# Moving the residual and the gated expert bias of a mixture-of-experts block into its last expert, and reordering the routing on TensorE

## The chip, the cores and the metric

The kernel runs on one core of one Trainium2 chip. The metric is the device time of one execution in microseconds (us). The kernel was timed in 3 runs, and one more execution was profiled. The engines are TensorE (PE; its weight loads are listed as PEld), VectorE (DVE), ScalarE (ACT), GpSimd (POOL) and SyncE (SP), whose queue issues nearly all transfers from HBM.

## What is computed

One layer of a diffusion backbone on 256 latent tokens and 256 context tokens of 1024 values, all float32. Cut to what the change touches:

```python
mod_l = silu_c @ w_mod + b_mod                      # 6 x 1024
sh1, sc1, g1, sh2, sc2, g2 = split(mod_l)
ml  = token_mixer(modulate(x, sh1, sc1), ...)       # scans, pooling, projections
xl  = layer_norm(alpha * x + g1 * ml, ln1_g, ln1_b)
h   = modulate(xl, sh2, sc2)
# mixture of experts: top 4 of 32, softmax over the chosen logits
logits = h @ router_w + router_b
gates  = softmax over top_k(logits, 4)              # 0 elsewhere
for e in range(32):
    gu  = h @ w1[e] + b1[e]
    a   = min(gu[:, :D], 7); l = clip(gu[:, D:], -7, 7)
    out += gates[:, e] * ((a * sigmoid(1.702 * a) * (l + 1)) @ w2[e] + b2[e])
xl = layer_norm(alpha * xl + g2 * out, ln2_g, ln2_b)
```

## The kernel before

**Weights.** All weights come through 20 blocks of SBUF of 1 MB each (128 partitions by 2048 floats): a ring of 12, and eight more that the first part of the kernel gives up when it no longer needs them (`donate`). The list `plan` fixes the order of the transfers: modulation, input projection, output projection, the last modulation part `("mod", 5, q)`, then for each expert in turn eight blocks of `w1` and, one expert later, four of `w2`. A block is freed when the last matmul that reads it has been written (`free`, `retire`), and each freed block lets SP's queue issue the next transfer of the plan. SP takes its transfers strictly in order, and each waits for the engines that last used its block.

**First part (L253 to L762).** Layer norms, modulation, scans, pooling and the output projection. Its instructions run on each engine in the order in which the code is written. It ends with the routing (L727 to L762): `project` is the output projection, `normalise(h)` the first layer norm of the token half h (it leaves the normalised tokens, without gain and bias, in `xn`), `turn1(h)` transposes `xn` on PE, `route(h)` makes from the transposed tokens `h2T` (modulated, four tiles by DVE and four by ACT), `xaT` (alpha times the first layer norm's output, eight tiles by ACT) and the router's logits `lp`; `top4a` and `top4b` pick the four experts on DVE (`selb`, `ge`), `place(h)` counts on PE where each token stands in its expert's queue, and `residual(h)` starts the four PSUM accumulators `acc[t][h]` with `xaT`, turned back by a matmul with the identity. `gemv(5)` computes the last modulation part g2; it is added to its bias row and spread to four groups of 32 partitions (`bp`, L751, copied to `g2s`).

**Experts (L764 to L1111).** Tokens go in groups of 32. The table `SEQ` says how many groups each of 32 experts, sorted by load, is given (56 groups in all); four groups make a page, and a pass takes one or two groups of one expert. A pass is: `gemm1` over eight `w1` blocks (with `hooks`, small pieces of other work after the k-th block, in PE's order), the bias `b1` by matmuls (L881), `swiglu` on DVE and ACT, and then, for the pass before it, `gemm2` over four `w2` blocks into the PSUM tile `py`, whose result DVE scales by `g2s` into `Y` (L929). `combine` adds a page's `Y` to `acc` with the gates as stationary operand. In pass 1 `arrange_a` and `arrange_b` sort the experts' maps, `arrange_b` also makes masked `b2` times g2 in `Y`, and `arrange_c` (L978, four matmuls of 128x512, right before `gemm2` of pass 0) adds gates times b2 to `acc`.

**End.** In the pass of the last expert (`p == NE - 1`), when the plan is empty, `spread` (L233) lays the second layer norm's gain and bias out over all partitions, `lngb`, by four pairs of matmuls and four ACT copies through one PSUM tile (`misc`, a single buffer). Then come `gemm1` of the last expert, `gemm2` of the last but one, `gemm2` of the last, the last `combine` and `last_norm`.

Of the kernel before, what the change touches and what calls it, by code (L numbers as in the profile page):

```python
# [18 lines left out]
P = 128  # L19
# [37 lines left out]
def hybrid(tc, a, out):  # L57
# [136 lines left out]
    AB = const.tile([P, 2, KD], F32, name="AB")  # L194
    aln = const.tile([P, 2, KD], F32, name="aln")
    posm = const.tile([P, 2, NE], F32, name="posm")
# [9 lines left out]
    keyc = const.tile([P, 2], F32, name="keyc")  # L206
    lnrow = const.tile([P, 2, T], F32, name="lnrow")
    pool.memset(lnrow, 0.0)
# [44 lines left out]
    with ExitStack() as px:  # L253
# [84 lines left out]

        gsel = sb.tile([GW, 3, P], F32, tag="gsel", name="gsel")
        for h in range(2):  # L340
# [24 lines left out]

        def gemv(v):
            gp = ps.tile([P, T], F32, tag="gv", name="gp")
            for q in range(4):
# [12 lines left out]
                free(("mod", v, q))  # L381
            return gp
# [46 lines left out]
        dve.tensor_scalar(hgb, col(C_GA, 16), 0.5, None, op0=ALU.mult)  # L429
        dve.tensor_scalar(aln, col(C_LG, 2 * KD).rearrange("p (i k) -> p i k", i=2), ALPHA, None, op0=ALU.mult)  # L430
        lam = col(C_LAM, 8)
# [181 lines left out]

        h2T, xaT = (block("aa")[:, D * i : D * i + D].rearrange("p (k t) -> p k t", k=KD) for i in range(2))
        eq = sb.tile([P, 2, NE], F32, name="eq")
# [31 lines left out]
        def route(h, trs):  # L647
            for j in range(KD):
                src = trs[j // 4][:, j % 4, :]
                if j >= 4:  # L650
                    act.activation(
                        h2T[:, j, :], src, AF.Identity, bias=AB[:, 1, j : j + 1], scale=AB[:, 0, j : j + 1]
                    )
                else:
                    dve.tensor_scalar(
                        h2T[:, j, :], src, AB[:, 0, j : j + 1], AB[:, 1, j : j + 1], op0=ALU.mult, op1=ALU.add
                    )
            for j in range(KD):
                src = trs[j // 4][:, j % 4, :]
                act.activation(  # L660
                    xaT[:, j, :], src, AF.Identity, bias=aln[:, 1, j : j + 1], scale=aln[:, 0, j : j + 1]
                )

            if h:
                lp = ps.tile([P, NE], F32, tag="gv", name="lp")
            else:
                lp = mm.tile([P, NE], F32, tag="mm", name="lp")
# [11 lines left out]
        def top4b(h):  # L679
            lh, gh, eh, ch, nh = lg[:, h, :], ge[:, h, :], eq[:, h, :], cum[:, h, :], ng[:, h : h + 1]  # L680
            v4 = mx[:, h, 3:4]
            dve.tensor_scalar(eh, lh, v4, None, op0=ALU.is_equal)
            dve.tensor_tensor_scan(ch, one, eh, 0.0, op0=ALU.mult, op1=ALU.add)
            dve.tensor_reduce(nh, gh, axis=AX.X, op=ALU.add)
            dve.tensor_scalar(nh, nh, -1.0, 4.0, op0=ALU.mult, op1=ALU.add)
            dve.scalar_tensor_tensor(ch, ch, nh, eh, op0=ALU.is_le, op1=ALU.mult)
            dve.tensor_tensor(gh, gh, ch, op=ALU.add)
            dve.tensor_copy(selb[:, h, :], gh)

# [24 lines left out]

        def residual(h):
            for j in range(KD):
                half, j4 = j // 4, j % 4
                pe.matmul(  # L718
                    acc[h][half][:, P * j4 : P * j4 + P],
                    xaT[:, j, :],  # L720
                    ident,
                    start=(j4 == 0),
                    stop=False,
                    skip_group_check=True,
                )

        project(0, (4, 5, 6, 7))  # L727
# [21 lines left out]
        bp = mm.tile([P, T], F32, tag="mm", name="bp")  # L749
        for c in range(4):  # L750
            pe.matmul(  # L751
                bp[32 * c : 32 * c + 32, :],
                ident[:, 32 * c : 32 * c + 1].to_broadcast([P, 32]),
                bgrow[:, 1, :],
                start=True,
                stop=True,
                skip_group_check=True,
            )
        act.activation(g2s, bp, AF.Copy)
        softmax_a(1)  # L760
        place(1)
        donate("aa")  # L762
    order = ExitStack()
# [57 lines left out]
    def maps(page):  # L821

        Pm = wk.tile([P, 2, P], F32, name="Pm")
# [67 lines left out]
    def swiglu(ph, av):  # L891
        sgm = wk.tile([P, T], F32, name="sgm")
# [37 lines left out]

    def combine(Y, PgT, t, h, lo=0, hi=512):

# [30 lines left out]
    def arrange_b():  # L963
# [4 lines left out]
        dve.tensor_copy(placed, so)  # L968
        ahead = page_maps(1)
        for c in range(4):  # L970
            dve.scalar_tensor_tensor(
                Y[:, T * c : T * c + T], b2, col(C_MASK + c), g2s, op0=ALU.mult, op1=ALU.mult
            )

    def arrange_c():
        for h in range(2):
            for t in range(2):
                pe.matmul(  # L978
                    acc[t][h],
                    GT[:, 2 + t],  # L980
                    Y[:, 512 * h : 512 * h + 512],
                    start=False,
                    stop=False,
                    skip_group_check=True,
                )
# [187 lines left out]
def _layout(inp):  # L1173
# [47 lines left out]
    def emb(n):  # L1221
# [42 lines left out]
```

## Time and profile before

| what | value |
|---|---|
| time, median of 3 runs | 1105.54 us (1105.21 to 1105.77) |
| time of the profiled execution | 1105.46 us |
| its span, first to last instruction | 1103.8 us |
| PE busy | 980.9 us, 89% of the span |
| DVE / ACT / POOL busy | 300.2 / 164.6 / 54.9 us |
| read from HBM | 442.25 MB, 402 GB/s over the span |
| mean granted TensorE clock | 0.954 of 2.4 GHz |
| chain of work that ended last | PE 55%, DMA 42% |

The span is 1.7 us shorter than the time of the same execution; what lies outside it is taken as fixed. Over most of the span the 16 DMA engines are at work throughout, and PE's busy time holds many waits for weights; the first fifth and the last 30 us are different stages with limits of their own, so shares over the whole span say little about them.

### The profile page before, as it was taken

To read this page: it belongs to the slowest core of one execution; us is meant where nothing else is said; L and a number is where in the kernel's file an instruction comes from. 1 tells how busy PE (TensorE), PEld (TensorE's weight loads), DVE (VectorE), ACT (ScalarE), POOL (GpSimd) and SP (SyncE) were. 2 spreads that over 40 slices of the span, in tenths; PEclk is the share of its full clock that TensorE was granted. 3 is DMA by queue.
4 is the path that set the end of the run, shared out by engine and by line. 5 is a ranking of instruction groups with operands and counts; after the bars stand their busy time and mean duration, and the time that the engine had idled before them with its cause. 6 is when DMAs were issued, how large, how long until landed. Compare 5 with 4: busy or idle time off the path is not lost.

```text
span 1103.8 us, 21803 instructions
## 1 busy us (share of the span) xinstructions
PE 980.9 (89%) x9237; PEld 420.1 (38%) x9238; DVE 300.2 (27%) x803; ACT 164.6 (15%) x347; POOL 54.9 (5%) x73
## 2 busy tenths in 40 slices
PE   7899999999999968699998897969999887999774
PEld 3356654434444313243433242324343233444222
DVE  4436562231313211213312112212221221223114
ACT  3245342101111000101010010000101010110011
POOL 2128200000000000000000000000000000000001
PEclk9899999999999989989998998989999998999886
DMA  9999689999999999999999999999999999999993
GB/s 366 355 404 374 260 348 379 376 422 424 422 424 423 423 424 424 424 425 424 423 424 424 424 423 424 423 425 423 424 422 425 425 423 424 425 423 414 424 422 135
DMA packets 89861, 444.76 MB, mean 403 GB/s; under 512 B 9304, under 2 KB 15576, under 8 KB 56992
## 3 DMA queue, kind: packets, MB, share of 16 engines
q1 hardware_dynamic: 89528, 443.01, 97.4%
q8 instruction: 74, 1.21, 0.4%
q10 hardware_dynamic: 232, 0.32, 0.1%
q14 instruction: 27, 0.22, 0.1%
HBM read 442.25 MB, written 1.05 MB: 402 GB/s over the span
## 4 chain that ended last, share of the span: by engine, by line
PE 55%; DMA 42%; DVE 2%; ACT 0%; issue 0%; ACTq 0%; SPq 0%; DVEq 0%
DMA blk<-in_w_dram 40%; PE ph L867 22%; PE py L916 12%; PE zp L458 5%; PE misc L847 3%; DMA blk<-in_w_mod_dram 2%; PE acc L604 2%; PE acc L933 2%; PE ph L881 2%; PE gp L373 1%; PE acc L488 1%; PE misc L906 1%; PE bp L233 1%; DMA cols<-in_cols_dram 0%; PE misc L857 0%; PE acc L718 0%
## 5 line engine op out<-in xcount | busy, mean ns | idle before, releaser
L867 PE MATMUL ph<-blk,xe 128*32 128x512 f32 x3584 | 430.4, 612 | 40.1 <-DMA blk<-in_w_dram 38.9
L916 PE MATMUL py<-blk,aT 128*32 128x256 f32 x3584 | 221.8, 400 | 54.5 <-DMA blk<-in_w_dram 49.8
L867 PEld LDWEIGHTS ph<-blk,xe 128*32 128x32 f32 x3584 | 104.2, 111 | 281.5 <-issue 176.3
L916 PEld LDWEIGHTS py<-blk,aT 128*32 128x32 f32 x3584 | 117.0, 115 | 170.8 <-issue 56.6
L929 DVE TENSOR_TENSOR Y<-py,g2s 32x256 f32<-32x256 f32 x224 | 94.2, 420 | 232.1 <-PE py L916 229.3
L894 DVE TENSOR_SCALAR av<-ph 128x256 f32<-128x256 f32 x56 | 23.6, 422 | 463.6 <-PE ph L881 463.6
L907 ACT ACTIVATE aT<-misc 128x256 f32<-128x256 f32 (+1 forms) x38 | 18.4, 485 | 386.2 <-PE misc L906 386.2
L850 ACT ACTIVATE xe<-misc,AB 128x128 f32<-128x128 f32 x108 | 40.7, 457 | 167.9 <-PE misc L847 167.9
L847 PEld LDWEIGHTS misc<-Pm,blk 128*128 128x128 f32 x432 | 51.4, 195 | 23.8 <-issue 23.8
L458 PE MATMUL zp<-blk 128*128 128x256 f32 (+1 forms) x192 | 59.2, 465 | 1.1 <-DVE blk L425 1.1
L847 PE MATMUL misc<-Pm,blk 128*128 128x128 f32 x432 | 56.5, 285 | 1.1 <-DVE Pm L826 1.1
L881 PE MATMUL ph<-b,SM 128*32 128x512 f32 x448 | 56.8, 609 | 0.0
L895 ACT ACTIVATE sgm<-av 128x256 f32<-128x256 f32 x56 | 23.3, 417 | 212.1 <-DVE av L894 212.1
L933 PE MATMUL acc<-Y,PgT 128*128 128x512 f32 (+1 forms) x120 | 51.9, 576 | 0.5 <-DVE Y L929 0.5
L1139 POOL TENSOR_TENSOR blk<-blk 128x512 f32<-128x512 f32 (+1 forms) x2 | 2.0, 995 | 941.7 <-ACT blk L1138 940.9
L458 PEld LDWEIGHTS zp<-blk 128*128 128x128 f32 x192 | 37.1, 195 | 22.6 <-issue 17.6
L933 PEld LDWEIGHTS acc<-Y,PgT 128*128 128x128 f32 x120 | 21.4, 189 | 31.3 <-issue 21.9
L881 PEld LDWEIGHTS ph<-b,SM 128*32 128x32 f32 x448 | 15.0, 114 | 35.7 <-issue 35.7
L604 PE MATMUL acc<-blk 128*128 128x512 f32 x64 | 27.8, 592 | 0.0
L897 DVE SCALAR_TENSOR_TENSOR av<-l,av 128x256 f32<-128x256 f32 x56 | 23.8, 426 | 10.8 <-ACT sgm L895 9.6
L373 PE MATMUL gp<-blk,csil 128*32 128x256 f32 x384 | 22.6, 381 | 2.1 <-DMA blk<-in_w_mod_dram 2.1
L906 PEld LDWEIGHTS misc<-ident,av 128*128 128x128 f32 x112 | 11.9, 144 | 32.9 <-issue 32.1
(214 smaller groups left out, 459.6 us busy)
## 6 DMA issues: line engine op xcount, KB each, us to landing
blk<-in_w_dram SPq DMA_DIRECT2D x383, 1024.0 KB, 19.6
blk<-in_w_mod_dram SPq DMA_DIRECT2D x23, 1024.0 KB, 10.6
blk<-in_w_in_dram SPq DMA_DIRECT2D x6, 1024.0 KB, 16.0
blk<-in_w_out_dram SPq DMA_DIRECT2D x4, 1024.0 KB, 5.3
blk<-in_ctx_dram SPq DMA_DIRECT2D x2, 512.0 KB
blk<-in_x_dram SPq DMA_DIRECT2D x2, 512.0 KB
blk<-in_w_mod_dram SPq DMA_DIRECT2D x2, 512.0 KB, 16.2
blk<-in_w_dram SPq DMA_DIRECT2D x2, 512.0 KB
```

What stands on the lines that cost most here:

```text
L373: pe.matmul(gp[32 * c : 32 * c + 32, :], csil[:, k, :], w[:, kk, T * c : T * c + T], start=(k == 0), stop=(k == KD - 1), skip_group_check= ...
L458: pe.matmul(zp[:, :n], w[:, k, P * half : P * half + P], hT(k)[:, :n], start=(k == 0), stop=(k == KD - 1))
L604: pe.matmul(acc[h][half], mixT[:, k, P * h : P * h + P], weight("out", k // 2)[:, k % 2, 512 * half : 512 * half + 512], start=(k == 4), s ...
L847: pe.matmul(gx[:, kk], xn[:, t, P * k : P * k + P], Pm[:, t], start=(t == 0), stop=(t == 1))
L850: act.activation(xe[:, k], gx[:, kk], AF.Identity, bias=AB[:, 1, k : k + 1], scale=AB[:, 0, k : k + 1])
L867: pe.matmul(ph[32 * c : 32 * c + 32], x[:, k], wv[:, :, c, :], start=(k == 0), stop=False, skip_group_check=True,)
L881: pe.matmul(ph[32 * c : 32 * c + 32], sel[c].to_broadcast([P, GS]), b1, start=False, stop=True, skip_group_check=True,)
L894: dve.tensor_scalar(av, ph[:, 0, :], 7.0, None, op0=ALU.min)
L897: dve.scalar_tensor_tensor(av, l1, 8.0, av, op0=ALU.min, op1=ALU.mult)
L916: pe.matmul(py[32 * c : 32 * c + 32, i], aT[:, i, k % 2, k // 2, :], W[k // 2][:, k % 2, T * c : T * c + T], start=(k == 0 and i == 0), st ...
L929: dve.tensor_tensor(dst[:, T * c : T * c + T], py[r, i], g2s[r], op=ALU.mult)
L933: pe.matmul(acc[t][h][:, lo:hi], PgT[:, P * t : P * t + P], Y[:, 512 * h + lo : 512 * h + hi], start=False, stop=False, skip_group_check=True,
```

## The change

- `residual` is no longer made in the routing: `xaT`, its sixteen ACT instructions, its sixteen matmuls of 128x128 and the table `aln` are gone. The accumulators are now started by the first `combine_all` (page 1, `start=True`).
- In the last expert's pass, four freed blocks are taken. `spread` first lays out the *first* layer norm's gain and bias (`ln1`, from two more rows of `lnrow`); DVE makes alpha times (`xn` * gain + bias) in token order, in four instructions of 128x1024 (`residual`), and then masked b2 times g2 into another block (`add_b2`, four of 128x256). Hooks of `gemm1` put the following into PE's order: after block 0 gates times b2 (four matmuls of 128x512), after blocks 2 and 4 the two `spread`s of the second layer norm's gain and bias, after block 5 the residual, by four matmuls of 128x512 with the identity.
- `arrange_c` and the b2 part of `arrange_b` are gone from pass 1.
- In the routing, three quarters of `gemv(5)` run where all of it ran; the fourth quarter runs after the second half's logits. The bias row of g2 is added by a matmul with the identity instead of by DVE, and ACT copies the sum to `g2r`. `top4b(0)` moves ahead of `turn1(1)` and `route(1)`, both `softmax_a` behind `top4b(1)`, and the spreading of g2 (`bp`) behind `place(1)`. `donate("aa")` moves to behind `route(1)`.
- `selb` is written by its own addition ahead of `ge`, not copied from it. `Pm` and `sgm` have one buffer instead of two, `gsel` shares a buffer, `lp` always comes from the pool `mm`.

```diff
-        g2p = gemv(5)
-        dve.tensor_tensor(bgrow[:, 1, :], g2p, bgrow[:, 1, :], op=ALU.add)
+        g2p = gemv(5, (0, 1, 2))
+        top4b(0)
         trs = turn1(1)
-        residual(0)
         lp = route(1, trs)
-        top4b(0)
+        donate("aa")
+        gemv(5, (3,), g2p)
+        pe.matmul(g2p, ident, bgrow[:, 1, :], start=False, stop=True, skip_group_check=True)
+        g2r = s2.tile([P, T], F32, tag="part", name="g2r")
+        act.activation(g2r, g2p, AF.Copy)
         place(0)
-        residual(1)
-        softmax_a(0)
         top4a(1, lp)
         top4b(1)
+        softmax_a(0)
+        softmax_a(1)
+        place(1)
...
+    def add_b2(Yb):
         for c in range(4):
             dve.scalar_tensor_tensor(
-                Y[:, T * c : T * c + T], b2, col(C_MASK + c), g2s, op0=ALU.mult, op1=ALU.mult
+                Yb[:, T * c : T * c + T], b2, col(C_MASK + c), g2s, op0=ALU.mult, op1=ALU.mult
             )
-    def arrange_c():
         for h in range(2):
             for t in range(2):
+                combine(Yb, GT[:, 2:4].rearrange("p t n -> p (t n)"), t, h)
+
+    def residual(ln1, R):
+        for h in range(2):
+            dve.scalar_tensor_tensor(R[:, h], xn[:, h], ALPHA, ln1[:, 0], op0=ALU.mult, op1=ALU.mult)
+            dve.scalar_tensor_tensor(R[:, h], ln1[:, 1], ALPHA, R[:, h], op0=ALU.mult, op1=ALU.add)
+
+    def add_residual(R):
+        for t in range(2):
+            for h in range(2):
                 pe.matmul(
+                    acc[t][h], ident, R[:, t, 512 * h : 512 * h + 512], start=False, stop=False, skip_group_check=True
                 )
...
-        if not plan and lngb is None:
-            lngb = block(slots.pop(0)).rearrange("p (i n) -> p i n", i=2)
+        if p == NE - 1:
+            tags = [slots.pop(0) for _ in range(4)]
+            lngb, ln1, y2 = (block(tag).rearrange("p (i n) -> p i n", i=2) for tag in tags[:3])
+            Yb = block(tags[3])[:, 0:D]
             for r in range(2):
-                spread(None, lnrow[:, r, :], wk, ps, "misc", lngb[:, r, :])
+                spread(None, lnrow[:, 2 + r, :], wk, ps, "misc", ln1[:, r, :])
+            residual(ln1, y2)
+            hooks[0] = lambda: add_b2(Yb)
+            for r in range(2):
+                hooks[2 + 2 * r] = lambda r=r: spread(None, lnrow[:, r, :], wk, ps, "misc", lngb[:, r, :])
+            hooks[5] = lambda: add_residual(y2)
```

PE in the routing, before: `lp` are the logits of the two halves, `gp` is `gemv(5)`, `tr` the transposes, `acc<-ident,blk` the residual, `pp` the counts, `bp` the spreading of g2.

```order
L669 MATMUL lp<-cols,blk 128x32 x8
L373 MATMUL gp<-blk,csil 32x256 x32
L643 MATMUL tr<-ident,blk 128x128 x8
L718 MATMUL acc<-ident,blk 128x128 x8
L669 MATMUL lp<-cols,blk 128x32 x8
L695 LDWEIGHTS tri
L695 MATMUL pp<-selb,tri 128x32
L718 MATMUL acc<-ident,blk 128x128 x8
L751 MATMUL bp<-bgrow,ident 32x256 x4
```

The same place now:

```order
L659 MATMUL lp<-cols,blk 128x32 x8
L372 MATMUL gp<-blk,csil 32x256 x24
L641 MATMUL tr<-ident,blk 128x128 x8
L659 MATMUL lp<-cols,blk 128x32 x8
L372 MATMUL gp<-blk,csil 32x256 x8
L722 MATMUL gp<-bgrow,ident 128x256
L685 LDWEIGHTS tri
L685 MATMUL pp<-selb,tri 128x32
L684 LDWEIGHTS one_305
```

Both residuals are gone, and the last quarter of `gp` with its bias now stands between the second logits and the first count; `bp` has moved out of this stretch, to behind the second count.

DVE in the same stretch, with the semaphores that each instruction waits for, down to the second half's logits (`lg<-lp,cols`): `blk<-tr,AB` are DVE's four tiles of the second half's `h2T`, and `eq` to `selb` is the pick of the first half's experts. Before:

```order
L655 TENSOR_SCALAR blk<-tr,AB 128x128 [waits PE_49]
L655 TENSOR_SCALAR blk<-tr,AB 128x128 x3
L682 TENSOR_SCALAR eq<-lg,mx 128x32
L683 SCALAR_TENSOR_TENSOR cum<-one,eq 128x32 [waits DVE_49]
L684 TENSOR_REDUCE ng<-ge 128x1
L685 TENSOR_SCALAR ng<-ng 128x1 [waits DVE_49]
L686 SCALAR_TENSOR_TENSOR cum<-cum,ng,eq 128x32 [waits DVE_49]
L687 TENSOR_TENSOR ge<-ge,cum 128x32 [waits DVE_49]
L688 CAST selb<-ge 128x32 [waits DVE_49]
L709 SCALAR_TENSOR_TENSOR posm<-pp,ge 128x32 [waits PE_49]
L238 TENSOR_SCALAR lg<-lg,mx 128x32
L674 TENSOR_TENSOR lg<-lp,cols 128x32
```

And now:

```order
L672 TENSOR_SCALAR eq<-lg,mx 128x32
L673 SCALAR_TENSOR_TENSOR cum<-one,eq 128x32 [waits DVE_49]
L674 TENSOR_REDUCE ng<-ge 128x1
L675 TENSOR_SCALAR ng<-ng 128x1 [waits DVE_49]
L676 SCALAR_TENSOR_TENSOR cum<-cum,ng,eq 128x32 [waits DVE_49]
L677 TENSOR_TENSOR selb<-ge,cum 128x32 [waits DVE_49]
L678 TENSOR_TENSOR ge<-ge,cum 128x32 [waits DVE_49]
L653 TENSOR_SCALAR blk<-tr,AB 128x128 [waits PE_49]
L653 TENSOR_SCALAR blk<-tr,AB 128x128 x3
L699 SCALAR_TENSOR_TENSOR posm<-pp,ge 128x32 [waits DVE_49,PE_49]
L664 TENSOR_TENSOR lg<-lp,cols 128x32
```

The pick of the first half (which stood behind the four tiles) is now ahead of them, and `posm`, which waits for PE's first count, still stands ahead of `lg`. Further down DVE's first `Pm`, which the first gather needs, now waits for PE and ACT too: its buffer lies where `g2r` lies, which `bp` reads.

PE at the end of pass 1, where the second row, the bias by `b1`, ends `gemm1` and `py` is `gemm2` of pass 0. Before:

```order
L867 MATMUL ph<-blk,xe 32x512 x8
L881 MATMUL ph<-b_72,SM 32x512 x8
L978 MATMUL acc<-Y,GT 128x512 x4
L916 MATMUL py<-blk,aT 32x256 x64
L867 MATMUL ph<-blk,xe 32x512 x16
```

And now:

```order
L846 MATMUL ph<-blk,xe 32x512 x8
L860 MATMUL ph<-b_72,SM 32x512 x8
L895 MATMUL py<-blk,aT 32x256 x64
L846 MATMUL ph<-blk,xe 32x512 x16
L885 MATMUL misc<-ident,av_1432 128x128 x2
```

`py` follows the bias at once; the four matmuls of L978 have gone to the last expert.

PE in the last expert's pass, before (`bp` is the spreading of the second layer norm's rows, `ph` is `gemm1`, `misc<-ident,av` a transpose, the first `py` is `gemm2` of the last expert but one):

```order
L233 MATMUL bp<-lnrow,ident 128x256 x8
L867 MATMUL ph<-blk,xe 32x512 x8
L906 MATMUL misc<-ident,av_7136 128x128 x2
L867 MATMUL ph<-blk,xe 32x512 x24
L881 MATMUL ph<-b_72,SM 32x512 x4
L916 MATMUL py<-blk,aT 32x256 x32
L906 MATMUL misc<-ident,av_7253 128x128 x2
L916 MATMUL py<-blk,aT 32x256 x32
```

Now (`bp` ahead of `ph` is the first layer norm's pair of rows; `acc<-blk,GT` is gates times b2, `acc<-blk,ident` the residual):

```order
L232 MATMUL bp<-lnrow,ident 128x256 x8
L846 MATMUL ph<-blk,xe 32x512 x4
L912 MATMUL acc<-blk,GT 128x512 x4
L846 MATMUL ph<-blk,xe 32x512 x4
L885 MATMUL misc<-ident,av_7096 128x128 x2
L846 MATMUL ph<-blk,xe 32x512 x4
L232 MATMUL bp<-lnrow,ident 128x256 x4
L846 MATMUL ph<-blk,xe 32x512 x8
L232 MATMUL bp<-lnrow,ident 128x256 x4
L846 MATMUL ph<-blk,xe 32x512 x4
L969 MATMUL acc<-blk,ident 128x512 x4
L846 MATMUL ph<-blk,xe 32x512 x8
```

Sixteen matmuls more stand inside `gemm1`, four of them after its first block; behind the last row the order is as before.

## Rows read from the trace of the kernel before

**Rows 1.** Stretches: length, TensorE's granted clock, DMA busy share, GB/s.

```profile
170.00:176.00 6.00, 1.00 0.71 268
210.00:220.00 10.00, 1.00 0.76 297
212.00:214.00 2.00, 1.00 1.02 430
214.00:216.00 2.00, 1.00 0.16 66
224.00:1064.00 840.00, 0.96 1.02 423
```

**Rows 2.** Chain that ended last: start us, us, engine, tile, line, count.

```profile
208.37 1.72 PE ph L881 x16
210.09 3.63 PE acc L978 x8
213.72 7.04 PE py L916 x128
...
275.95 3.45 PE py L916 x64
```

**Rows 3.** Timeline of SP's queue at the gap: start us, us, what is issued.

```profile
215.65 0.33 SPq L156 DMA_DIRECT2D blk<-in_w_dram  x1
```

**Rows 4.** Timeline of the routing, PE and DVE: start us, us, operation.

```profile
153.99 3.66 PE L373 MATMUL gp<-blk,csil 128*32 128x256 f32 x64
...
157.30 0.24 DVE L677 TENSOR_SCALAR ge<-lg,mx 128x32 f32<-128x32 f32 x1
...
158.27 1.37 DVE L655 TENSOR_SCALAR blk<-tr,AB 128x128 f32<-128x128 f32 x4
...
160.29 1.87 PE L669 MATMUL lp<-cols,blk 128*128 128x32 f32 x16
...
162.49 0.18 DVE L674 TENSOR_TENSOR lg<-lp,cols 128x32 f32<-128x32 f32 x1
...
163.99 0.64 PE L751 MATMUL bp<-bgrow,ident 128*32 128x256 f32 x8
...
166.12 2.02 PE L847 MATMUL misc<-Pm,blk 128*128 128x128 f32 x16 [1.12 <-DVE Pm L826]
```

**Rows 5.** Timeline of the last expert's pass and the end: start us, us, operation [idle <-releaser].

```profile
1051.81 0.60 ACT L234 ACTIVATE blk<-bp 128x512 f32<-128x512 f32 x1 [1.22 <-PE bp L233]
...
1055.34 1.92 PE L867 MATMUL ph<-blk,xe 128*32 128x512 f32 x16
1055.44 0.60 ACT L234 ACTIVATE blk<-bp 128x512 f32<-128x512 f32 x1 [1.22 <-PE bp L233]
...
1057.19 0.44 PE L906 MATMUL misc<-ident,av 128*128 128x128 f32 x2
...
1077.60 1.94 PE L916 MATMUL py<-blk,aT 128*32 128x256 f32 x16 [1.39 <-DMA blk<-in_w_dram]
...
1079.63 1.73 DVE L929 TENSOR_TENSOR Y<-py,g2s 32x256 f32<-32x256 f32 x4 [7.05 <-PE py L916]
...
1081.46 6.73 PE L916 MATMUL py<-blk,aT 128*32 128x256 f32 x64 [1.30 <-DVE Y L929]
...
1087.55 0.16 PEld L916 LDWEIGHTS py<-blk,aT 128*32 128x32 f32 x8 [0.54 <-DMA blk<-in_w_dram]
```

**Rows 6.** DVE's groups by shape: count, busy us, mean ns.

```profile
L898 DVE TENSOR_TENSOR av<-av,sgm 128x256 f32<-128x256 f32 x56 | 23.8, 425 | 1.9
...
L629 DVE TENSOR_TENSOR blk<-sub,blk 128x512 f32<-128x512 f32 x2 | 1.4, 692 | 0.1
```

**Rows 7.** Stretches of the end: length, PE busy us and count, granted clock, DMA share, GB/s.

```profile
1059.80:1063.10 3.30, 1.39 (x12) 1.00 1.03 429
1063.20:1069.90 6.70, 5.35 (x28) 0.50 1.02 423
...
1076.90:1087.00 10.10, 8.10 (x70) 0.50 0.56 231
```

More of the change, by code (lines that the diff above doesn't have):

```diff
@@ L194, in hybrid @@
     AB = const.tile([P, 2, KD], F32, name="AB")
-    aln = const.tile([P, 2, KD], F32, name="aln")
     posm = const.tile([P, 2, NE], F32, name="posm")
@@ L206, in hybrid @@
     keyc = const.tile([P, 2], F32, name="keyc")
-    lnrow = const.tile([P, 2, T], F32, name="lnrow")
+    lnrow = const.tile([P, 4, T], F32, name="lnrow")
     pool.memset(lnrow, 0.0)
@@ L337, in turn0 @@
                     dve.tensor_copy(dst, tr)
-        gsel = sb.tile([GW, 3, P], F32, tag="gsel", name="gsel")
+        gsel = s2.tile([GW, 3, P], F32, tag="a2", name="gsel")
         for h in range(2):
@@ L362, in hybrid, with gemv @@
         norm0(1)
-        def gemv(v):
-            gp = ps.tile([P, T], F32, tag="gv", name="gp")
-            for q in range(4):
+        def gemv(v, qs=range(4), gp=None):
+            gp = gp or ps.tile([P, T], F32, tag="gv", name="gp")
+            for q in qs:
                 w = weight("mod", v, q)
@@ L429, in hybrid @@
         dve.tensor_scalar(hgb, col(C_GA, 16), 0.5, None, op0=ALU.mult)
-        dve.tensor_scalar(aln, col(C_LG, 2 * KD).rearrange("p (i k) -> p i k", i=2), ALPHA, None, op0=ALU.mult)
         lam = col(C_LAM, 8)
@@ L612, in project @@
                 free(*(("out", k // 2) for k in ks[::2]))
-        h2T, xaT = (block("aa")[:, D * i : D * i + D].rearrange("p (k t) -> p k t", k=KD) for i in range(2))
+        h2T = block("aa")[:, 0:D].rearrange("p (k t) -> p k t", k=KD)
         eq = sb.tile([P, 2, NE], F32, name="eq")
@@ L657, in route @@
                     )
[L658 to L667, printed above, removed]
+            lp = mm.tile([P, NE], F32, tag="mm", name="lp")
             for k in range(KD):
@@ L686, in top4b @@
             dve.scalar_tensor_tensor(ch, ch, nh, eh, op0=ALU.is_le, op1=ALU.mult)
+            dve.tensor_tensor(selb[:, h, :], gh, ch, op=ALU.add)
             dve.tensor_tensor(gh, gh, ch, op=ALU.add)
-            dve.tensor_copy(selb[:, h, :], gh)
         def place(h):
@@ L713, in place @@
                 dve.tensor_copy(keyc[:, 1:2], pp[:, 2, 0:1])
[L715 to L725, printed above, removed]
         project(0, (4, 5, 6, 7))
@@ L753, in hybrid @@
                 ident[:, 32 * c : 32 * c + 1].to_broadcast([P, 32]),
-                bgrow[:, 1, :],
+                g2r,
                 start=True,
@@ L759, in hybrid @@
         act.activation(g2s, bp, AF.Copy)
-        softmax_a(1)
-        place(1)
-        donate("aa")
     order = ExitStack()
@@ L821, in maps @@
     def maps(page):
-        Pm = wk.tile([P, 2, P], F32, name="Pm")
+        Pm = wk.tile([P, 2, P], F32, name="Pm", bufs=1)
         for to, n, p, lo in runs(page):
@@ L891, in swiglu @@
     def swiglu(ph, av):
-        sgm = wk.tile([P, T], F32, name="sgm")
+        sgm = wk.tile([P, T], F32, name="sgm", bufs=1)
         l1 = wk.tile([P, T], F32, name="l1", bufs=1)
@@ L929, in gemm2, with combine @@
                 dve.tensor_tensor(dst[:, T * c : T * c + T], py[r, i], g2s[r], op=ALU.mult)
-    def combine(Y, PgT, t, h, lo=0, hi=512):
+    def combine(Y, PgT, t, h, lo=0, hi=512, start=False):
         pe.matmul(
@@ L936, in combine @@
             Y[:, 512 * h + lo : 512 * h + hi],
-            start=False,
+            start=start,
             stop=False,
@@ L940, in combine, with combine_all @@
         )
-    def combine_all(Y, PgT):
+    def combine_all(Y, PgT, start=False):
         for h in range(2):
             for t in range(2):
-                combine(Y, PgT, t, h)
+                combine(Y, PgT, t, h, start=start)
     def arrange_a():
@@ L969, in arrange_b @@
         ahead = page_maps(1)
+    def add_b2(Yb):
         for c in range(4):
             dve.scalar_tensor_tensor(
-                Y[:, T * c : T * c + T], b2, col(C_MASK + c), g2s, op0=ALU.mult, op1=ALU.mult
+                Yb[:, T * c : T * c + T], b2, col(C_MASK + c), g2s, op0=ALU.mult, op1=ALU.mult
             )
-    def arrange_c():
         for h in range(2):
             for t in range(2):
-                pe.matmul(
[L979 to L984, printed above, removed]
+                combine(Yb, GT[:, 2:4].rearrange("p t n -> p (t n)"), t, h)
[6 more added lines that the diff above has]
+            for h in range(2):
+                pe.matmul(
+                    acc[t][h], ident, R[:, t, 512 * h : 512 * h + 512], start=False, stop=False, skip_group_check=True
                 )
@@ L1061, in hybrid @@
     act.activation(wk.tile([P, 1], F32, name="sgm0", bufs=1), zero, AF.Sigmoid)
-    lngb, PgT, done = None, None, None
+    PgT, done = None, None
     of_page = [[n for n, (p, gs) in enumerate(passes) if gs[0] // 4 == page] for page in range(NG // 4)]
@@ L1101, in hybrid @@
         if at == 1 and back is not None:
-            combine_all(Y, back)
-        if n == 1:
-            arrange_c()
+            combine_all(Y, back, page == 1)
         if done:
@@ L1116, in hybrid @@
     mv = wk.tile([P, 2, 4], F32, name="mv", bufs=1)
-    y2 = block(slots.pop(0)).rearrange("p (t n) -> p t n", t=2)
+    slots.extend((tags[1], tags[3]))
     def moments(t):
@@ L1239, in _layout @@
         "b2": g["exp_b2"][0].reshape(NE, 4, T).transpose(1, 0, 2).reshape(P, T),
-        "lnrow": np.stack([g[n][0].reshape(4, T) for n in ("ln2_g", "ln2_b")], axis=1),
+        "lnrow": np.stack([g[n][0].reshape(4, T) for n in ("ln2_g", "ln2_b", "ln1_g", "ln1_b")], axis=1),
         "w_mod": g["w_mod"][0],
```

## Prediction, made before the changed kernel ran

> **What bounds the kernel now.** I read the stretches of DMA first. From 224 to 1064 us the transfers run at 423 GB/s without a break [rows 1]: there the time is the plan's bytes, and nothing that an engine saves counts unless it lets a transfer start earlier while the DMA engines stand idle. So the change is worth what it does to idle DMA ahead of 224 us, and what it does behind the last transfers. Two idle places bear on it. From 170 to 176 us the rate is 268 GB/s: all blocks are full, and the first experts' matmuls, which start after the routing, must free one. From 210 to 220 us it is 297: 430 still at 212 to 214, 66 at 214 to 216 [rows 1]. The chain of waits names the owner of the second hole: PE does L881, then L978 for 3.63 us, then `gemm2` of pass 0 from 213.72 [rows 2], and SP's next transfer goes out at 215.65 [rows 3], when that `gemm2` has used up its first `w2` block. Behind 1064 us the timeline shows the last expert: PE waits for weights, and its last step waits for DMA at 1087.55, at the end of the last `gemm2` [rows 5]. So the end too is set by transfers before the change, but PE has little air there.
>
> **Pass 1: L978 and b2 leave.** Their four matmuls stand on PE between the end of `gemm1` and `gemm2` of pass 0, so `gemm2`, and with it the next free block, comes 3.63 us earlier [rows 2]. What is late next is the stream itself: without the hole it would run on, and the transfer at 215.65 would go out at 212.0, when data still flow at 430 GB/s [rows 1]. The hole is worth 10 us x (1 - 297/423) = 3.0 us; bounds: 3.6 us if the whole PE piece counts, and 0 if another wait keeps the block. I take 3.0, the measured idle. DVE's four instructions for b2 were hidden behind gathers and give nothing.
>
> **Routing.** Counted up to the first gather at 166.12 [rows 4], because SP's hole at 170 to 176 moves one to one with it. Ahead of the second transposes `gemv` loses a quarter of 3.66 us, 0.9 us. DVE now does the first half's pick, seven instructions of some 0.2 us, right behind `top4a(0)`, which ends at 157.30 + 0.24, and ahead of its four `h2T` tiles. So these start not at 158.27 but at 157.54 + 1.4 = 158.9, and with 1.37 us end at 160.3. The second logits took until 160.29 + 1.87 = 162.16; now they lack only their last five steps at 160.3 (5/8 of 1.87 = 1.2), so they end near 161.5, 0.7 earlier: the removed residual would have given more, but the pick takes it. Then PE does a quarter of `gemv` (0.9) and the bias matmul (128x256, half of a quarter of 3.63: 0.45) ahead of the first count (0.1 to 0.2), and DVE's `posm` waits for that count with `lg` behind it: `lg` at 163.0 to 163.1 instead of 162.49. From there `selb` gets one step (0.2) earlier, so the second count starts 0.3 to 0.4 late; and DVE's first `Pm` now waits for `bp` (0.64 us, which was early before), another 0.1 to 0.2. Sum: **0.5 us later**. Bounds: 0.4 earlier (if the 0.7 at the logits lasts and most of the new PE piece hides), 1.4 later (all of the new piece). ACT's missing sixteen instructions lay beside PE's work and give nothing. `donate("aa")` now precedes the last quarter of `gemv` in SP's queue: its transfer goes out when the second logits are read, near 161.5, the next near 162.4. Behind them nothing is due before the first experts' matmuls, and the stream still has blocks queued then, so this costs nothing.
>
> **The stream** therefore runs 3.0 - 0.5 = 2.5 us earlier from 220 us on, and so do the experts, which wait for it. Single buffers for `Pm` and `sgm` add waits on DVE's and ACT's own earlier instructions only; in order they are over.
>
> **The last expert.** Counted in the old times, from where `spread` begins; all of it then shifts by -2.5. `spread` costs what it did. The change is behind it. PE does block 0 from 1055.34 to 1056.2 (8 of 16 records in 1.92 us [rows 5]), then, in order, stands before gates times b2, which needs DVE: the gain is laid out at 1051.81 + 0.60 = 1052.4, the bias at 1055.44 + 0.60 = 1056.04 [rows 5]. A two-input instruction takes 425 ns for 256 and 692 for 512 [rows 6], so about 1.23 us for 1024. The second of the four starts at 1056.05, the fourth ends at 1059.75, and two of the b2 instructions (0.42 each) end at 1060.6. So PE stands idle for **4.4 us**; the weights meanwhile arrive. From 1060.6 on it must do, without a wait for DMA: four matmuls 128x512 (3.6, as L978), seven blocks of `gemm1` (7 x 0.86 = 6.0), the transpose (0.4), two spreads (each two halves of 0.9 with a wait of 0.9 between for the single PSUM buffer, from the ACT pitch of (1055.44 - 1051.81)/2 = 1.8: 2 x 2.7 = 5.4), the residual (3.5), b1 (half of L881's 1.72: 0.9), `gemm2` of the last but one (3.45 [rows 2]), DVE's 1.73 on `py` before that single buffer is free, with latency 1.9, and the last `gemm2` (3.45). Sum 28.6: it ends at 1089.2. Before, the last `gemm2` ended at 1081.46 + 6.73 = 1088.19. So **1.0 us late** if PE's clock stays up. The last `w2` lands by 1087.55 and no longer decides.
>
> **The clock.** At 1059.8 to 1063.1 PE was busy for 1.39 of 3.30 us, and then the granted clock was 0.50, 1.2 GHz, for 6.7 us although PE was busy for 5.35 of them [rows 7]. A gap of 4.4 us with nothing in it is more idle than that, so I expect a slow stretch behind it. Up to 6.7 us long, of which about 2.5 lie in the gap and in the spreads' waits, it does 4.2 us of work at half speed: **2.1 us**. Bounds: 0, and 5.0 for one like that of 10.1 us at 1076.9 [rows 7]. [...] What was gained is no relief elsewhere: the old last `gemm2` ran at 0.50 up to 1087 [rows 7] behind its weights, and the last `combine` and the norm are the same.
>
> **Sum**, on the profiled execution's 1105.46 us (span 1103.8; the median of the runs, 1105.54, is 0.08 more, and I let that go): -3.0 + 0.5 + 1.0 + 2.1 = +0.6: **1106.1 us**. A measurement of this kernel tells about 0.2%, 2.2 us, from no change.
>
> **Rivals.** (A) *PE keeps up at the end.* If the wide DVE instructions run faster than two inputs of 512 suggest (half as long: 0.6 us each, so the gap shrinks by 1.8) and the clock stays, the last `gemm2` again ends with its weights, and the stream's gain shows: 1105.46 - 2.5 = 1103.0. For it: nothing else runs on DVE and POOL there. Against: the 692 ns are for just such operands, and the idle gap stays over 2.5 us. [...] (B) *The clock stays down to the end.* The mechanism is the gap at gates times b2, and a second idle time of 1.9 us where `py` waits for DVE between the two last `gemm2`: with a slow stretch at each, the price is 2.1 to 3 for the first and half of the last 6.9 us, some 2.5 to 3.4, for the second, together 5.5 instead of 2.1: 1109.5. It is measurably slower once the clock costs more than 2.2 + 2.5 - 1.0 = 3.7 us. For it: the old end had two slow stretches, with fewer long gaps [rows 7]. Against: `gemm1` and `gemm2` are now dense from 1060.6 on. (C) *The hole at 214 is not closed*, because another wait holds the block of `gemm2` of pass 0, or the late first gather eats it. Then 0 instead of -3.0: 1109.1. For it: 1.4 us of the routing's bound fall on the same path. Against: no other work stands between L881 and `gemm2` in the new order.
>
> **Chances.** Forecast (between 1103.5 and 1107.7 with its terms' bounds) 0.58; A 0.14; B 0.21; C 0.07. Faster by over 0.2% (below 1103.3): A and a little of the forecast's lower edge, 0.16. Slower by over 0.2% (above 1107.7): B, C and little of the upper edge, 0.28. Within 0.2%: 0.56. The range takes in A's centre and most of B: 1102.7 to 1109.2, leaving out 0.2.
>
> **What would show it.** In the changed profile: no stretch near 66 GB/s between 210 and 220 us, SP's transfer there about 3 us earlier, and 423 GB/s through; the first gather at 166.3 to 167; in the last expert an idle time of PE of some 4 us ended by DVE ahead of the matmuls of gates times b2, a clock of 0.50 shortly behind it, and a last `gemm2` that waits for DVE or runs through, no longer for DMA. The forecast is wrong if the first gather comes at 165 (routing gains), if that idle time is under 2 us, if the clock stays at 1.00 from 1055 to the end, or if the last `gemm2` still waits for weights.

## The result, and the profile after

The changed kernel takes 1131.46 us (median of 6 runs, 1126.10 to 1133.06) against 1104.65 for the kernel before, measured beside it: a ratio of 1.0229, 95% interval 1.0203 to 1.0255. It is 2.3% slower; the forecast was 1106.1, the range 1102.7 to 1109.2. The profiled execution took 1126.10 us, with a span of 1124.3, 20.5 more than before. It is the shortest of the six (the others: 1126.38 and 1131.19 to 1133.06), so what follows accounts for 20.5 of the 26.8 us between the medians.

The stretches of DMA come first, as they did before the change (the row of the page of after: GB/s in 40 slices of the span; then the stretches of [rows 1] in after: length, granted clock, DMA busy share, GB/s):

```profile
GB/s 356 349 393 391 268 350 330 416 416 417 414 416 417 415 416 416 416 417 416 416 416 417 416 416 416 416 416 416 416 415 417 417 415 417 416 411 410 416 399 100
```

The stretches:

```profile
170.00:176.00 6.00, 0.80 0.41 163
210.00:220.00 10.00, 1.00 1.02 422
212.00:214.00 2.00, 1.00 1.02 426
214.00:216.00 2.00, 1.00 1.03 422
224.00:1064.00 840.00, 0.95 1.02 416
```

The hole at 214 us is gone (422 GB/s for 297). The one at 170 us is deeper (163 for 268). And the steady stretch, where before the DMA engines moved 423 GB/s, moves 416 with the same busy share of 1.02 and the same bytes. The transfers themselves are slower, from one end of the stream to the other: in the DMA records of this stretch a packet (one record there) of 8192 bytes takes 315.2 ns on average, where it took 309.9 before, and one of 4096 bytes 163.3 for 159.5. 840 us at 423 GB/s take 840 x 423/416 = 854.1 us at 416.

The routing (timeline of after, PE and DVE; answers to [rows 4]):

```profile
154.55 2.80 PE L372 MATMUL gp<-blk,csil 128*32 128x256 f32 x48
...
159.43 1.36 DVE L653 TENSOR_SCALAR blk<-tr,AB 128x128 f32<-128x128 f32 x4
...
159.89 2.26 PE L659 MATMUL lp<-cols,blk 128*128 128x32 f32 x16 [1.52 <-DVE blk L653]
...
162.08 1.94 PE L372 MATMUL gp<-blk,csil 128*32 128x256 f32 x16
...
163.94 1.22 PE L722 MATMUL gp<-bgrow,ident 128*128 128x256 f32 x2
165.34 0.18 DVE L664 TENSOR_TENSOR lg<-lp,cols 128x32 f32<-128x32 f32 x1
...
168.95 3.65 PE L826 MATMUL misc<-Pm,blk 128*128 128x128 f32 x16 [0.85 <-DVE Pm L805]
```

`gp`, the first work that the new order touches, begins 0.56 us later than before. In the profiles of all runs it begins between 152.66 and 154.75 us, so this much is not the routing's and is subtracted. The last quarter of `gp` takes 1.94 us, where a quarter of the 3.66 in [rows 4] is 0.9, and the first gather 3.65 where it took 2.02. That is half speed, and the clock says so: 0.53 from 162 to 164 us, 0.74 from 168 to 170 and 0.50 from 170 to 172 (longer stretches of after: length, busy us of PE, PEld, DVE, ACT and POOL, granted clock, DMA share, GB/s):

```profile
158.00:164.00 6.00, 4.48 (x37) 2.90 (x35) 2.62 (x12) 1.51 (x4) 0.00 (x0) 0.84 1.00 413
164.00:170.00 6.00, 3.10 (x29) 2.17 (x29) 4.28 (x27) 2.43 (x5) 0.00 (x0) 0.78 1.02 412
170.00:174.00 4.00, 4.00 (x28) 3.81 (x28) 2.07 (x14) 1.23 (x4) 0.00 (x0) 0.70 0.62 245
```

Before, the clock was 1.00 in all of it: from 170 to 176 us [rows 1], and ahead of that (the first two stretches in the kernel before):

```profile
158.00:164.00 6.00, 6.00 (x58) 5.88 (x55) 4.33 (x22) 5.21 (x13) 0.00 (x0) 1.00 0.99 413
164.00:170.00 6.00, 4.88 (x56) 4.19 (x56) 5.21 (x35) 2.61 (x8) 0.00 (x0) 1.00 1.03 423
```

The first gather now ends at 172.60; before it ended at 168.14 [rows 4]. Of these 4.46 us, 0.56 is the later start: the routing costs 3.9.

The last expert (timeline of after; answers to [rows 5]):

```profile
1072.12 0.60 ACT L233 ACTIVATE blk<-bp 128x512 f32<-128x512 f32 x1 [1.22 <-PE bp L232]
...
1076.28 1.66 DVE L953 SCALAR_TENSOR_TENSOR blk<-b,cols,g2s 128x256 f32<-128x256 f32 x4
...
1077.21 5.22 PE L912 MATMUL acc<-blk,GT 128*128 128x512 f32 x8 [4.14 <-DVE blk L953]
...
1099.56 3.64 PE L895 MATMUL py<-blk,aT 128*32 128x256 f32 x64
...
1105.09 3.66 PE L895 MATMUL py<-blk,aT 128*32 128x256 f32 x64 [1.52 <-issue]
```

Two stretches of it in after, with the columns of the last ones:

```profile
1076.90:1080.30 3.40, 3.09 (x4) 1.52 (x5) 1.04 (x3) 0.00 (x0) 0.00 (x0) 0.50 1.02 418
1080.30:1117.80 37.50, 29.35 (x241) 13.86 (x239) 11.88 (x26) 6.79 (x12) 2.85 (x2) 1.00 0.54 216
```

PE stands idle 4.14 us for DVE's b2, and the matmuls behind it run at 0.50; then the clock is 1.00 to 1117.8 us. The last bias copy of the first `spread` begins at 1072.12, at 1055.44 before [rows 5]: 16.68 us late. The last `gemm2` ends at 1108.75, at 1088.19 before: 20.56 late. So the end itself costs 3.9, and 16.7 come from ahead of it: 0.6 of a later start, +3.9 routing, -3.0 hole, and some 15, the remainder, of the slower stream (14.1 by the 840 us above).

### The profile page after: what moved, and what is told of

It is laid out like the page before. It is cut to its first block, busy times and chain, and to the rows that moved or that the text cites. A ratio compares the mean times of both kernels' runs of the same rounds, so it can differ in the third digit from the quotient of the medians.

```text
span 1124.3 us, 21771 instructions
## 1 busy us (share of the span) xinstructions
PE 986.2 (88%) x9231; PEld 422.7 (38%) x9232; DVE 304.3 (27%) x805; ACT 161.8 (14%) x336; POOL 55.3 (5%) x73
## 4 chain that ended last, share of the span: by engine, by line
PE 50%; DMA 46%; DVE 2%; issue 1%; ACT 1%; SPq 0%; DVEq 0%; ACTq 0%
DMA blk<-in_w_dram 43%; PE ph L846 20%; PE py L895 10%; PE zp L456 5%; PE misc L826 3%; PE acc L912 2%; DMA blk<-in_w_mod_dram 2%; PE acc L602 2%; PE ph L860 2%; PE acc L486 1%; PE gp L372 1%; PE misc L885 1%; PE bp L232 1%; DMA blk<-in_ctx_dram 0%; ACT blk L233 0%
## 5 line engine op out<-in xcount | busy, mean ns | idle before, releaser
L895 PE MATMUL py<-blk,aT 128*32 128x256 f32 x3584 | 218.1, 395 | 57.5 <-DMA blk<-in_w_dram 55.9
L877 DVE TENSOR_TENSOR av<-av,sgm 128x256 f32<-128x256 f32 x56 | 23.8, 425 | 1.9
```

The source lines that it names most:

```text
L895: pe.matmul(py[32 * c : 32 * c + 32, i], aT[:, i, k % 2, k // 2, :], W[k // 2][:, k % 2, T * c : T * c + T], start=(k == 0 and i == 0), st ...
```

## The experiments

**What slows every transfer?** The change removes `aln` (64 bytes a partition) and gives `lnrow` two more rows (2048 bytes). Both lie ahead of the 20 weight blocks in SBUF, so all blocks move by 1984 bytes: in the allocation of the built programs the first began at 29184 (57 x 512) and now begins at 31168 (60 x 512 + 448). The suspicion (ALIGN) is that a transfer into a block is slower when the block starts at such an address. The rivals: the larger `lnrow` array in device memory (DRAM), and the new order of work (WORK). Five runs (e1, e2, e4, e9, e10) only put an unused tile behind `lnrow`, which shifts the blocks, and with them whatever else is laid out behind `lnrow`; the only new instruction is its memset. n is 16, 16, 32, 64 and 112 floats.

```diff
     pool.memset(lnrow, 0.0)
+    pad = const.tile([P, n], F32, name="pad")
+    pool.memset(pad, 0.0)
```

One run enlarges the array in device memory alone, in the kernel before:

```diff
-        plan.append((("lnrow", c), a["lnrow"][c : c + 1]))
+        plan.append((("lnrow", c), a["lnrow"][c : c + 1, 0:2]))
...
-        "lnrow": np.stack([g[n][0].reshape(4, T) for n in ("ln2_g", "ln2_b")], axis=1),
+        "lnrow": np.stack([g[n][0].reshape(4, T) for n in ("ln2_g", "ln2_b", "ln1_g", "ln1_b")], axis=1),
```

> The changed kernel with 64 bytes per partition put behind lnrow, so that the weight blocks begin in SBUF at 31232 (61 times 512) instead of 31168. Theory ALIGN (the rate of the stream fell because the blocks' start is no longer a multiple of 512 or 128 bytes): 423 GB/s again from 224 us on, last-but-one expert's gemm2 some 15 us earlier, 1110 to 1117 us. Rival DRAM (the larger lnrow array moved the weights in device memory) and rival WORK (the changed order of work slows the stream): 416 GB/s and 1126 to 1133 us, as the changed kernel.

> The kernel before with 64 bytes per partition put behind lnrow, so that the weight blocks begin at 29248 (57 times 512 plus 64). ALIGN: 416 GB/s instead of 423 and 15 to 22 us more, 1119 to 1127 us. DRAM and WORK: 423 GB/s and 1104 to 1106 us, as before.

> The kernel before with the four-row lnrow array in device memory (16 KB in place of 8 KB, as in the changed kernel), of which it still loads two rows; the blocks in SBUF stay at 29184. ALIGN and WORK: 423 GB/s and 1104 to 1106 us. DRAM: 416 GB/s and 1119 to 1127 us.

> The kernel before with 128 bytes per partition put behind lnrow: blocks at 29312 (57 times 512 plus 128). If ALIGN holds with a step of 128 bytes or less: 423 GB/s and 1104 to 1106 us; if it holds with a step of 256 or 512 bytes: 416 GB/s and 1119 to 1127 us. DRAM and WORK: 1104 to 1106 us.

> The kernel before with 256 bytes per partition put behind lnrow: blocks at 29440 (57 times 512 plus 256). If the step that counts is 512 bytes: 416 GB/s and 1119 to 1123 us, as at 64 and 128. If it is 256 bytes: 423 GB/s and 1104 to 1106 us.

> The kernel before with 448 bytes put behind lnrow: blocks at 29632 (57 times 512 plus 448), the changed kernel's own remainder. If each remainder but 0 costs the same: 1120 to 1124 us, 16 us over before, as at 64 and 128. If the changed kernel's remainder costs more than these (it stood 20 us above its aligned copy e1, its profiled run 15): 1125 to 1128 us.

| kernel | blocks start at, modulo 256 | GB/s, 224 to 1064 us | time | ratio to before (95%) |
|---|---|---|---|---|
| before | 0 | 423 | 1104.65 to 1106.07 | 1 |
| e9: before, 256 more | 0 | 423 | 1105.50 | 1.0002 (0.9992 to 1.0012) |
| e3: larger array only | 0 | 423 | 1105.22 | 0.999 (0.998 to 1.000) |
| e2: before, 64 more | 64 | 416 | 1122.13 | 1.015 (1.0133 to 1.0167) |
| e4: before, 128 more | 128 | 416 | 1121.47 | 1.014 (1.0123 to 1.0157) |
| e10: before, 448 more | 192 | 416 | 1123.91 | 1.0172 (1.0153 to 1.0191) |
| changed kernel | 192 | 416 | 1131.46 | 1.0229 (1.0203 to 1.0255) |
| e1: changed, 64 more | 0 | 423 | 1111.63 | 1.005 (1.0033 to 1.0067) |

The same stretch of e2, the kernel before with 64 bytes more (length, clock, DMA share, GB/s):

```profile
224.00:1064.00 840.00, 0.95 1.02 416
```

Of e9, with 256 bytes more:

```profile
224.00:1064.00 840.00, 0.97 1.02 423
```

And of e1, the changed kernel with 64 bytes more:

```profile
224.00:1064.00 840.00, 0.96 1.02 423
```

Sixty-four unused bytes take the kernel before to 416 GB/s and the changed kernel back to 423. That decides for ALIGN: DRAM falls with e3, and WORK with e1 and e2. At the starts tried the step is 256 bytes: a start at 256 is fast, starts at 64, 128 and 192 behind a multiple are slow, by 1.4 to 1.7% of the time. The DMA records of the same stretch agree: packets of 8192 bytes take 309.9 to 310.1 ns in before, e3, e9 and e1, and 314.8, 314.5 and 315.0 at 64, 128 and 192 (e2, e4, e10); packets of 4096 bytes take 159.5 to 159.6 ns and 163.1 to 163.3. So the price does not grow with the bytes that lie between the multiple below and the start: at remainder 64 as at 192 the larger packets take 1.6% longer (314.8 and 315.0 ns for 309.9). Why such a start makes the transfers slower is not shown by these runs.

One thing stays open: e1 is 19.8 us faster than the changed kernel, while e10, with the same remainder, is 18 us slower than before. The changed kernel's runs fall into two groups, two near 1126.2 (the profiled one among them) and four at 1131 to 1133. Against the first group e1 gains 14.6 us, which is about what the stream accounts for; what makes the four others some 5 to 7 us longer is not known, and the profile shows none of them. Single runs of e6, e7, e11 and e12 too lie 2 to 6 us above the median of their kernel.

**What makes the routing long?** All further runs but e8 stand on e1. Two theories: CLOCK, that PE, without the residual's matmuls, waits more and is granted half the clock (0.50); ORDER, that the new sequence is a longer chain at any clock. e5 puts spare matmuls where the residual's were, e6 restores the old order without them, e12 does both. The sums of the spare matmuls are never read.

e5, and in the old order e12:

```diff
+        def spare(h):
+            for j in range(KD):
+                half, j4 = j // 4, j % 4
+                pe.matmul(acc[h][half][:, P * j4 : P * j4 + P], ident, ident,
+                    start=(j4 == 0), stop=False, skip_group_check=True)
...
         trs = turn1(1)
+        spare(0)
         lp = route(1, trs)
...
         place(0)
+        spare(1)
```

e6 (e12 has `spare(0)` behind `turn1(1)` and `spare(1)` behind `place(0)` in it):

```diff
-        g2p = gemv(5, (0, 1, 2))
-        top4b(0)
+        g2p = gemv(5)
+        dve.tensor_tensor(bgrow[:, 1, :], g2p, bgrow[:, 1, :], op=ALU.add)
         trs = turn1(1)
         lp = route(1, trs)
-        donate("aa")
-        gemv(5, (3,), g2p)
...
+        top4b(0)
         place(0)
+        softmax_a(0)
         top4a(1, lp)
         top4b(1)
...
         act.activation(g2s, bp, AF.Copy)
+        softmax_a(1)
+        place(1)
+        donate("aa")
```

> e1 (the changed kernel with aligned blocks, 1111.63 us) with 16 spare matmuls of ident by ident into acc at the two places of the routing where the residual matmuls stood before; their sums are never read, since the first combination begins acc anew. Theory CLOCK (the routing takes 3.9 us longer because TensorE, with less to do, falls to 1.2 GHz): clock 1.00 instead of about 0.75 between 158 and 178 us, the first expert's gemm1 2 to 3 us earlier, 1108.5 to 1110 us. Rival ORDER (the longer chain of the new order itself, whatever the clock): 1111 to 1113 us.

> e1 with the routing's order of before (the whole last modulation part, then turn, route, top 4 and place; the bias added by VectorE), but without the residual matmuls, so that TensorE still has less to do. ORDER: 2 to 4 us gone, 1107.5 to 1109.5 us. CLOCK: the clock still falls in the routing and 1111 to 1113 us stay, or half of it is back at most (1110 us).

> e6 (aligned, the routing's order of before, no residual) with e5's 16 spare matmuls at the residual's places: the fourth of the four cases of order and work. CLOCK: clock 1.00 through the routing, the first gather in 2.0 us instead of 3.75, the first gemm1 some 1.1 us earlier than in e6 from the end of the projection, 1107 to 1108.5 us. If the order alone had given the 2.9 us: 1108.5 to 1109.5 us, as e6.

| | time | ratio to before (95%) | from the start of `gp` to the first `gemm1` |
|---|---|---|---|
| before (old order, residual) | 1104.65 to 1106.07 | 1 | 153.99 to 170.26: 16.3 us |
| e1 (new order, nothing) | 1111.63 | 1.0050 (1.0033 to 1.0067) | 153.69 to 173.99: 20.3 |
| e5 (new order, spare) | 1108.71 | 1.0033 (1.0021 to 1.0045) | 152.66 to 169.82: 17.2 |
| e6 (old order, nothing) | 1108.76 | 1.0039 (1.0022 to 1.0056) | 153.97 to 171.35: 17.4 |
| e12 (old order, spare) | 1107.81 | 1.0031 (1.0017 to 1.0044) | 152.94 to 169.19: 16.3 |

Stretches of e1, which e5 is to be held against:

```profile
158.00:164.00 6.00, 4.47 (x36) 3.33 (x37) 2.31 (x10) 1.61 (x6) 0.00 (x0) 0.85 0.99 411
164.00:170.00 6.00, 3.60 (x30) 2.71 (x30) 4.93 (x30) 1.93 (x4) 0.00 (x0) 0.50 1.03 421
```

The same of e5:

```profile
158.00:164.00 6.00, 5.81 (x56) 4.88 (x55) 2.70 (x14) 1.75 (x3) 0.00 (x0) 1.00 1.01 418
164.00:170.00 6.00, 5.15 (x59) 4.34 (x62) 5.46 (x36) 2.33 (x8) 0.00 (x0) 1.00 1.02 416
```

The last quarter of `gp`, its bias and the first gather in e1:

```profile
161.22 1.08 PE L374 MATMUL gp<-blk,csil 128*32 128x256 f32 x16
162.23 1.22 PE L724 MATMUL gp<-bgrow,ident 128*128 128x256 f32 x2
...
167.71 3.75 PE L828 MATMUL misc<-Pm,blk 128*128 128x128 f32 x16 [0.85 <-DVE Pm L807]
```

And in e5:

```profile
160.19 1.07 PE L374 MATMUL gp<-blk,csil 128*32 128x256 f32 x16
161.19 0.70 PE L737 MATMUL gp<-bgrow,ident 128*128 128x256 f32 x2
...
165.69 2.02 PE L842 MATMUL misc<-Pm,blk 128*128 128x128 f32 x16 [0.85 <-DVE Pm L821]
```

With 16 matmuls that compute nothing, PE is busy for 5.81 and 5.15 us of the two stretches and the clock stays at 1.00, where in e1 it fell to 0.85 and 0.50. The quarter of `gp` is as short in e1 as in e5 (in the changed kernel it took 1.94); the bias takes 0.70 us instead of 1.22 and the gather 2.02 instead of 3.75. The routing is 3.1 us shorter. The time is 2.9 us less by the medians and 1.9 by the ratios, whose intervals overlap: it is the traces, one execution of each kernel, that carry this. That is CLOCK. e6 says that order counts too, but through the clock: in the old order, without spare work, the clock falls as well (stretch of e6):

```profile
164.00:170.00 6.00, 4.88 (x33) 4.49 (x28) 3.66 (x25) 1.09 (x4) 0.00 (x0) 0.54 1.02 414
```

but there mostly the gathers run slow on the path (3.75 us for the first). From the four cases: the new order costs 17.2 - 16.3 = 0.9 us at full clock; without work in the residual's place the routing is 3.1 us longer in the new order and 1.1 in the old. The 1.1 is a net: up to the first gather e6 is 0.9 us shorter than e12 (11.25 us from the start of `gp`, for 12.11), which is what the matmuls had cost there, and from the gather to `gemm1` it is 2.0 longer (6.13 for 4.14). My expectation of e6 had CLOCK leave 1110 at best; it was too simple, since the two act on one another.

**The end.** e7 makes masked b2 times g2 on DVE ahead of the residual, in a block that is free earlier (the lines leave `add_b2`):

```diff
-            lngb, ln1, y2 = (block(tag).rearrange("p (i n) -> p i n", i=2) for tag in tags[:3])
-            Yb = block(tags[3])[:, 0:D]
+            lngb, ln1, y2 = (block(tag).rearrange("p (i n) -> p i n", i=2) for tag in (tags[3], tags[1], tags[2]))
+            Yb = block(tags[0])[:, 0:D]
+            for c in range(4):
+                dve.scalar_tensor_tensor(
+                    Yb[:, T * c : T * c + T], b2, col(C_MASK + c), g2s, op0=ALU.mult, op1=ALU.mult
+                )
```

> e1 with the four VectorE instructions that make gates times b2 ahead of the residual's four in the last expert (and ahead of the spreading of ln1's rows), in a block that is free earlier. Theory PE (TensorE's queue sets the end, and its wait of 4.1 us for VectorE lies on the path): the wait gone, 1107.5 to 1109.6 us. Rival (the last weights or the last turn take its place): over 1110.5 us.

1106.73 us, 4.9 less than e1 by the medians and 3.2 by the ratios to the kernel before (1.0021, 1.0010 to 1.0031, for 1.0050, 1.0033 to 1.0067). That is about PE's wait of 4.14 us; a little under the 1107.5 that was expected at the least. Timeline of e7:

```profile
1056.86 1.06 PE L848 MATMUL ph<-blk,xe 128*32 128x512 f32 x8
1057.86 3.70 PE L914 MATMUL acc<-blk,GT 128*128 128x512 f32 x8
...
1084.21 3.23 PE L897 MATMUL py<-blk,aT 128*32 128x256 f32 x56 [1.53 <-issue]
1087.68 0.64 PE L897 MATMUL py<-blk,aT 128*32 128x256 f32 x8 [0.24 <-DMA blk<-in_w_dram]
```

And the stretch of these matmuls (columns as in the routing's stretches):

```profile
1056.80:1062.00 5.20, 5.20 (x25) 1.75 (x24) 3.59 (x3) 0.60 (x1) 0.00 (x0) 1.00 1.01 418
```

The matmuls follow the first block at once and take 3.70 us instead of 5.24 in e1: without the idle time the clock is 1.00 here, where behind it the changed kernel had 0.50. And the last `gemm2` waits for weights again: PE has caught up.

**Is the rest worth anything?** e11 is e1, e5 and e7 together; e8 is the kernel before with gates times b2 alone moved, ahead of `spread` as in e7 (residual, routing and const tiles stay):

```diff
-        for c in range(4):
-            dve.scalar_tensor_tensor(
-                Y[:, T * c : T * c + T], b2, col(C_MASK + c), g2s, op0=ALU.mult, op1=ALU.mult
-            )
...
-        if n == 1:
-            arrange_c()
...
+            btag = slots.pop(0)
+            Yb = block(btag)[:, 0:D]
+            for c in range(4):
+                dve.scalar_tensor_tensor(
+                    Yb[:, T * c : T * c + T], b2, col(C_MASK + c), g2s, op0=ALU.mult, op1=ALU.mult
+                )
+            hooks[0] = lambda: add_b2(Yb)
```

> The changed kernel with all three mended: aligned blocks (e1), spare matmuls in the routing (e5) and gates times b2 ahead of the residual (e7). If the three are separate and add: 1131.5 less 19.8, 2.9 and 4.9, 1103 to 1105 us, at or under the 1105.5 of before. If routing and end share the same time (what the stream gains early the end loses): 1105.5 to 1107 us.

> The kernel before with one part of the change alone: gates times b2 is made and added in the last expert, instead of at the second. Residual, routing and const tiles as before (blocks at 29184). If the hole in the stream at 214 us is worth the 3.0 us that it lacks, and the eight matmuls of 3.6 us find room at the end: 1101.5 to 1103.5 us. Rival (the end is TensorE's, and the matmuls push it out by what the stream gained): 1104.3 to 1106 us.

e11: 1104.45 us, ratio 0.9999 (0.9985 to 1.0014). Within the noise the three mends add (by medians 1131.5 - 19.8 - 2.9 - 4.9 = 1103.9; by ratios 1.0229 - 0.0179 - 0.0017 - 0.0029 = 1.0004) and bring the change to no difference. The hole's gain is used up: 0.9 us by the routing, which takes 17.2 us in e11 as in e5 (152.86 to 170.02); that the fuller end takes the rest is inferred, not shown. e8: 1103.21, ratio 0.9984 (0.9975 to 0.9992), the only version ahead of the kernel before, by 0.16%. Stretches of e8:

```profile
210.00:220.00 10.00, 1.00 1.01 424
224.00:1064.00 840.00, 0.96 1.02 423
```

The hole is closed, and the end carries the four matmuls.

## Why the prediction was wrong, step by step

- **The failed step** is the one headed "the stream": that it "therefore runs 3.0 - 0.5 = 2.5 us earlier from 220 us on, and so do the experts". It took the 423 GB/s of [rows 1] as a constant that the change cannot touch, and so the largest part of the result, 14 to 20 us (e1 against the changed kernel: 13.6 by the spans of the profiled executions, 19.8 by the medians), is in no term and in no rival: 416 GB/s ran where it had 423. Even all the bounds that it named for its terms, taken together, reach only from 1102.5 to 1112.9 us, which is wider than the 1103.5 to 1107.7 that it gives for them. The diff showed the cause: `aln` gone and `lnrow` doubled, ahead of the blocks. I costed the instructions of these tiles, not their bytes: 2048 - 64 = 1984 = 7 x 256 + 192.
- **The hole at 214 us**: right. 422 GB/s where there were 297, and in e8 the part alone.
- **Routing, +0.5 (bounds -0.4 to 1.4)**: the term that was mis-sized, 3.9. Its pieces up to the second logits hold: DVE's tiles were laid out for 158.9 and came at 159.43 - 0.56 = 158.87. The order at full clock costs 0.9, inside the bounds. What is missing is the clock, 3.1 (e1 against e5): the removed residual was taken as a gain that the pick eats, and that PE thereby idles, [1.52 <-DVE blk L653] in front of the logits, was not carried on to the clock, though the same argument was made for the end.
- **The last expert, +1.0, and the clock, +2.1**: right in mechanism and nearly in size: an idle time of 4.14 us (4.4 forecast) ended by DVE, whose wide instructions took the 1.23 us laid out for them, 0.50 behind it, and a last `gemm2` that waits for no weights; 3.9 in all for 3.1. The slow stretch is shorter than I took it (3.4 us for 6.7). The traces give the clock as a share of full speed alone; no run shows a figure in GHz. Rival A did not come; of B, the second slow stretch did not come.
- **Without the alignment** the kernel would be e1, 1.005 (1.0033 to 1.0067), that is, 1111 us on the 1105.5 of before: above my range too in the middle of its interval (1109.1 to 1112.9), by the routing's clock. C did not come. B's own time, 1109.5, lay just outside the range that was said to take in most of B.
- **Its signs.** None of the four signs of being wrong came, though it was wrong: the first gather came late, at 168.95 for 166.3 to 167, and the sign that touches the failed step, "423 GB/s through", stood among those of being right.

## What to carry to other kernels

Add up the bytes of every small tile that a change adds or removes ahead of the buffers of a stream: here 64 unused bytes cost the kernel before 16 us (e2), and the sign in a profile is a rate that is a little lower all along the stream (416 GB/s for 423) at the same DMA busy share (1.02). Before matmuls are taken out of a stretch that waits on dependencies, ask what becomes of TensorE's clock there: here it was 1.00 with such work (e5, e12) and without it 0.85 and 0.50 in the two stretches from 158 to 170 us in the new order (e1), 0.90 and 0.54 in the old (e6). In the old order the removed work had cost 0.9 us ahead of the first gather and its absence cost 2.0 behind it; in the new order its absence cost 3.1. And when work is put into TensorE's order behind work of another engine, put that engine's part for it first; the same eight instructions on DVE in another order were worth 3 to 5 us (e7 against e1).

## What I had not expected of the hardware

- The rate of the weight stream went with where its blocks start in SBUF, modulo 256 bytes, and, at the four remainders tried, only with whether that is 0: 423 GB/s at 0 (before, e9, e3, e1), 416 at 64 (e2), at 128 (e4) and at 192 (e10 and the changed kernel).
- Sixteen useless matmuls of 128x128 made the routing 3.1 us shorter and the kernel 2 to 3 us faster, with the granted clock at 1.00 where it had been 0.85 and 0.50 (e5 against e1).
